# Rotary position embedding: fp16 tiles summed on TensorE, or fp32 tiles worked in place by four engines

## The chip, the cores and the metric

One core of a Trainium2 chip runs the kernel. The metric is device time in microseconds of one execution. The kernel before has a median of 165.84 us over 3 runs (165.72 to 165.95).

## What is computed

`x` is fp32 of shape (16, 512, 1024): 16 batches, 512 positions, and 16 heads of 64 values side by side. `cos` and `sin` are (512, 32). Each head's 64 values are two halves of 32, and every position's halves are rotated:

```python
x = x.reshape(batch, seq, num_heads, head_dim)
x1, x2 = x[..., :half_dim], x[..., half_dim:]
cos, sin = cos[None, :, None, :], sin[None, :, None, :]
rotated = np.concatenate([x1 * cos - x2 * sin, x1 * sin + x2 * cos], axis=-1)
```

The output is fp32 of the same size, so 33.55 MB are read and 33.55 MB written. For each element that is one product with cosine, one product of the other half with plus or minus sine, and one sum.

## The kernel before

A batch is one tile: position `4p + kk` lies on partition `p`, so a partition holds 4 positions, 16 KB in fp32. Set-up (L51 to L62) makes a 128x128 fp16 identity, loads cosine and sine from SP (L56, L57) and casts them to fp16 tables on DVE, sine twice: negated for the first half of a head, plain for the second.

The loop over `bo` (L82) takes two batches at a time. POOL issues one DMA that loads both and casts them to fp16 on the way (L84); this runs on the software queue, q0. Then for each batch:

- DVE multiplies the tile by cosine into `A` (L90), and the tile with its halves swapped (`swap_view`, a view that steps backwards by 32) by the signed sine into `Bt` (L92). Each is one operation over 128x4096 in fp16.
- PE adds the two: for each of 8 chunks of 512 columns an identity matmul of `A` (L101) and one of `Bt` (L102) accumulate in one PSUM bank, in fp32.
- ACT copies each chunk from PSUM into `o_sb` (L103), in fp32.
- SP stores `o_sb`, 2 MB, on the hardware queue, q1 (L105).

The order on each engine is the scheduler's, from the dependences and the buffers: 3 of `x_sb` (two batches each), 2 of `A` and `Bt`, 3 of `o_sb`, 4 PSUM banks. POOL's fourth load waits until DVE has read the first `x_sb`; ACT's copies for the fourth batch wait until the first store has landed.

Of the kernel before, what the change touches and what calls it, by code (L numbers as in the profile page):

```python
# [1 line left out]

# [5 lines left out]

FP32 = mybir.dt.float32  # L10
FP16 = mybir.dt.float16
ALU = mybir.AluOpType


@with_exitstack
def kernel(
    ctx: ExitStack,
    tc: tile.TileContext,
    x: bass.AP,
    cos: bass.AP,  # L20
    sin: bass.AP,
    num_heads: bass.AP,
    out: bass.AP,
):
    nc = tc.nc
    P = nc.NUM_PARTITIONS
    batch, seq, dim = x.shape
    nh = num_heads
    head_dim = dim // nh
    half = head_dim // 2  # L30

    KK = seq // P
    assert P * KK == seq
    FREE = KK * dim
    CH = 512
    assert FREE % CH == 0
    BP = 2
    assert batch % BP == 0

    x_v2 = x.rearrange("(bo bi) (p kk) d -> bo p bi kk d", bi=BP, kk=KK)  # L40
    out_v = out.rearrange("b (p kk) h d -> b p kk (h d)", kk=KK)
    cos_v = cos.rearrange("(p kk) j -> p kk j", kk=KK)
    sin_v = sin.rearrange("(p kk) j -> p kk j", kk=KK)

    fixed = ctx.enter_context(tc.tile_pool(name="fixed", bufs=1))
    xin = ctx.enter_context(tc.tile_pool(name="xin", bufs=3))
    tmp = ctx.enter_context(tc.tile_pool(name="tmp", bufs=2))
    orez = ctx.enter_context(tc.tile_pool(name="orez", bufs=3))
    psum = ctx.enter_context(tc.tile_pool(name="psum", bufs=4, space=bass.MemoryType.PSUM))

    ident = fixed.tile([P, P], FP16)  # L51
    make_identity(nc, ident)

    cos_sb = fixed.tile([P, KK, half], FP32)
    sin_sb = fixed.tile([P, KK, half], FP32)
    nc.sync.dma_start(out=cos_sb, in_=cos_v)  # L56
    nc.sync.dma_start(out=sin_sb, in_=sin_v)  # L57
    cos16 = fixed.tile([P, KK, half], FP16)
    sns16 = fixed.tile([P, KK, 2, half], FP16)
    nc.vector.tensor_copy(out=cos16, in_=cos_sb)  # L60
    nc.vector.tensor_scalar_mul(out=sns16[:, :, 0, :], in0=sin_sb, scalar1=-1.0)  # L61
    nc.vector.tensor_copy(out=sns16[:, :, 1, :], in_=sin_sb)  # L62

    cosb = bass.AP(
        tensor=cos16.tensor,
        offset=cos16.offset,
        ap=[cos16.ap[0], [half, KK], [0, nh * 2], [1, half]],
    )
    snsb = bass.AP(
        tensor=sns16.tensor,  # L70
        offset=sns16.offset,
        ap=[sns16.ap[0], [2 * half, KK], [0, nh], [1, 2 * half]],
    )

    def swap_view(x_sb):
        return bass.AP(
            tensor=x_sb.tensor,
            offset=x_sb.offset + half,
            ap=[x_sb.ap[0], [head_dim, KK * nh], [-half, 2], [1, half]],
        )  # L80

    for bo in range(batch // BP):  # L82
        x_sb = xin.tile([P, BP, KK, dim], FP16)
        nc.gpsimd.dma_start(out=x_sb, in_=x_v2[bo])  # L84
        for bi in range(BP):
            b = bo * BP + bi
            xb = x_sb[:, bi]

            A = tmp.tile([P, KK, dim], FP16, name="A")
            nc.vector.tensor_tensor(out=A, in0=xb, in1=cosb, op=ALU.mult)  # L90
            Bt = tmp.tile([P, KK, dim], FP16, name="Bt")
            nc.vector.tensor_tensor(out=Bt, in0=swap_view(xb), in1=snsb, op=ALU.mult)  # L92

            o_sb = orez.tile([P, KK, dim], FP32)
            Aflat = A.rearrange("p kk d -> p (kk d)")
            Bflat = Bt.rearrange("p kk d -> p (kk d)")
            oflat = o_sb.rearrange("p kk d -> p (kk d)")
            for c in range(FREE // CH):
                sl = slice(c * CH, (c + 1) * CH)
                ps = psum.tile([P, CH], FP32)  # L100
                nc.tensor.matmul(out=ps, lhsT=ident, rhs=Aflat[:, sl], start=True, stop=False)  # L101
                nc.tensor.matmul(out=ps, lhsT=ident, rhs=Bflat[:, sl], start=False, stop=True)  # L102
                nc.scalar.copy(out=oflat[:, sl], in_=ps)  # L103

            nc.sync.dma_start(out=out_v[b], in_=o_sb)  # L105


# [1 line left out]
_INS = ['x', 'cos', 'sin', 'num_heads']  # L109
_OUTS = [((16, 512, 16, 64), 'float32')]  # L110
#: Inputs that are plain numbers.
_NUMBERS = {'num_heads': 16}


# [26 lines left out]
```

## Time and profile before

| What | Value |
|---|---|
| Median of 3 runs | 165.84 us |
| Span of the profiled execution | 164.1 us (its time outside the span is not given) |
| Busy: PE, DVE, ACT, POOL | 88.6, 72.5, 68.7, 6.5 us |
| Largest wait on DVE | 41.3 us for the load of `x_sb` |
| Largest wait on ACT | 58.5 us for stores out of `o_sb` |
| From issue to landing: load of two batches, store of one | 40.3 us, 23.5 us (medians) |
| Last store: issued, span's end | 152.38 us, 164.1 us |

The span runs from the first instruction to the last. A transfer is counted in GB/s by the bytes that it writes; the line on HBM counts what was read and written there. The DMA line gives the mean busy share of 16 DMA engines in 40 slices of 4.1 us, in tenths. Stretches of the span are given as start and end in microseconds.

### The profile page before, as it was taken

What the parts mean: (1) busy time and instruction counts of PE and PEld (TensorE: products, weight loads), DVE (VectorE), ACT (ScalarE), POOL (GpSimd) and SP (SyncE); (2) the same over time, 40 slices, a digit from 0 to 9 for tenths busy, and PEclk for the clock granted to TensorE, in tenths of its full rate; (3) what the DMA queues carried; (4) which work ended last, traced back from release to release, by engine and by line L of the source; (5) the groups of instructions that cost most, each with busy time, mean ns of one, the idle gap of its engine ahead of it and who ended that gap; (6) DMA issues with size and microseconds to landing.
All of it is one profiled execution on the core that took longest, in us unless ns stands there. A gap on an engine that the chain in (4) does not pass through costs nothing.

```text
span 164.1 us, 814 instructions
## 1 busy us (share of the span) xinstructions
PE 88.6 (54%) x256; PEld 31.5 (19%) x256; DVE 72.5 (44%) x35; ACT 68.7 (42%) x129; POOL 6.5 (4%) x14
## 2 busy tenths in 40 slices
PE   0000599940954908639195491954919559986000
PEld 0000133310311302213032130311303123331000
DVE  1005979904880073900929037280733707950000
ACT  3000289811805409145080541806428075798100
POOL 7000010010001000010000100000000000000000
PEclk9999999998586585865858658586585855999955
DMA  5999999999999999999999999999999999999992
GB/s 90 196 218 222 220 208 180 290 332 326 312 312 330 324 298 336 306 308 346 310 312 312 326 328 306 326 308 326 326 316 316 304 403 423 413 435 443 423 423 92
DMA packets 4772, 50.51 MB, mean 308 GB/s; under 512 B 416, under 2 KB 672, under 8 KB 672
## 3 DMA queue, kind: packets, MB, share of 16 engines
q0 software_dynamic: 2176, 16.78, 49.7%
q1 hardware_dynamic: 2592, 33.69, 48.8%
q8 instruction: 2, 0.03, 0.1%
q14 instruction: 2, 0.02, 0.0%
HBM read 33.69 MB, written 33.55 MB: 410 GB/s over the span
## 4 chain that ended last, share of the span: by engine, by line
DMA 71%; PE 11%; ACT 6%; DVE 3%; issue 1%; ACTq 0%; POOL 0%; POOLq 0%; DVEq 0%
DMA out_dram<-o_sb 63%; DMA x_sb<-in_x_dram 8%; ACT o_sb L103 6%; PE ps L102 6%; PE ps L101 6%; DVE A L90 1%; DVE Bt L92 1%; ACTq L136 0%; POOL ident masks.py:197 0%; ACTq L103 0%; POOLq masks.py:199 0%; DVEq L90 0%; POOLq L122 0%
## 5 line engine op out<-in xcount | busy, mean ns | idle before, releaser
L103 ACT COPY o_sb<-ps 128x512 f32<-128x512 f32 x128 | 67.4, 609 | 82.9 <-DMA out_dram<-o_sb 58.5
L101 PE MATMUL ps<-A,ident 128*128 128x512 f16 x128 | 65.4, 519 | 60.8 <-ACT o_sb L103 43.6
L90 DVE TENSOR_TENSOR A<-x_sb,cos 128x4096 f16<-128x4096 f16 x16 | 36.7, 2291 | 69.9 <-DMA x_sb<-in_x_dram 41.3
L102 PE MATMUL ps<-Bt,ident 128*128 128x512 f16 x128 | 62.9, 506 | 1.6 <-DVE Bt L92 1.6
L92 DVE TENSOR_TENSOR Bt<-x_sb,sns 128x4096 f16<-128x4096 f16 x16 | 36.6, 2285 | 0.0
L102 PEld LDWEIGHTS <-ident 128*128 128x128 f16 x128 | 15.6, 122 | 87.0 <-issue 83.7
L101 PEld LDWEIGHTS <-ident 128*128 128x128 f16 x128 | 15.8, 124 | 32.1 <-issue 23.5
L84 POOL DMA_DIRECT2D x_sb<-in_x_dram x8 | 5.8, 730 | 83.9 <-DVE Bt L92 83.6
L103 ACT ACT_TABLE_LOAD x1 | 1.3, 1283 | 0.7 <-PEq L122 0.7
L60 DVE CAST cos<-cos_sb 128x128 f16<-128x128 f32 x1 | 0.2, 227 | 2.6 <-DMA cos_sb<-in_cos_dram 2.6
L61 DVE TENSOR_SCALAR sns<-sin_sb 128x128 f16<-128x128 f32 x1 | 0.5, 509 | 0.6 <-DMA sin_sb<-in_sin_dram 0.6
L62 DVE CAST sns<-sin_sb 128x128 f16<-128x128 f32 x1 | 0.4, 434 | 0.0
masks.py:199 POOL TENSOR_SCALAR_AFFINE_SELECT ident<-ident 128x128 f16<-128x128 f16 x1 | 0.3, 304 | 0.1
masks.py:197 POOL MEMSET ident<- 128x128 f16 x1 | 0.2, 205 | 0.3 <-POOLq L122 0.3
L122 POOL MEMSET const-float32-0.0<- 128x1 f32 x1 | 0.1, 93 | 0.2 <-issue 0.2
L122 POOL MEMSET const-bfloat16-1.0<- 128x1 bf16 x1 | 0.1, 95 | 0.0
L122 POOL MEMSET const-uint8-127<- 128x1 uint8 x1 | 0.1, 95 | 0.0
L122 POOL MEMSET const-float32-1.0<- 128x1 f32 x1 | 0.1, 93 | 0.0
## 6 DMA issues: line engine op xcount, KB each, us to landing
out_dram<-o_sb SPq DMA_DIRECT2D x16, 2048.0 KB, 23.5
x_sb<-in_x_dram POOLq DMA_DIRECT2D x8, 2048.0 KB, 40.3
cos_sb<-in_cos_dram SPq DMA_DIRECT2D x1, 64.0 KB, 1.8
sin_sb<-in_sin_dram SPq DMA_DIRECT2D x1, 64.0 KB, 2.2
```

The costliest lines, as they stand in the source:

```text
L60: nc.vector.tensor_copy(out=cos16, in_=cos_sb)
L61: nc.vector.tensor_scalar_mul(out=sns16[:, :, 0, :], in0=sin_sb, scalar1=-1.0)
L62: nc.vector.tensor_copy(out=sns16[:, :, 1, :], in_=sin_sb)
L84: nc.gpsimd.dma_start(out=x_sb, in_=x_v2[bo])
L90: nc.vector.tensor_tensor(out=A, in0=xb, in1=cosb, op=ALU.mult)
L92: nc.vector.tensor_tensor(out=Bt, in0=swap_view(xb), in1=snsb, op=ALU.mult)
L101: nc.tensor.matmul(out=ps, lhsT=ident, rhs=Aflat[:, sl], start=True, stop=False)
L102: nc.tensor.matmul(out=ps, lhsT=ident, rhs=Bflat[:, sl], start=False, stop=True)
L103: nc.scalar.copy(out=oflat[:, sl], in_=ps)
L122: nc = _bacc.Bacc("TRN2", target_bir_lowering=False, num_devices=1)
```

## The change

The new kernel keeps fp32 from end to end and writes the result over the input tile.

- **Tiles.** Two batches make one tile of 128 partitions: 64 partitions for each batch, 8 positions ("rows" of 1024 values) per partition, 32 KB. There are 8 tiles, and 5 buffers for them.
- **Transfers.** All are issued from SP on the hardware queue, in an order written out by hand: both tables, tile 0 in two halves (rows 0 to 3, rows 4 to 7), tiles 1 to 4, stores of tiles 0 to 2, loads of tiles 5 to 7, stores of tiles 3 to 6, the store of tile 7 in two halves. Each load of the second round waits for a store out of its buffer.
- **Tables.** Cosine and sine are loaded once to 64 partitions. PE copies them to both halves of 128 partitions in PSUM, through selection matrices that DVE makes from the identity (three fp32 matmuls). `sns_ps` and `cos_ps` stay in PSUM and are read there by DVE; ACT copies both to SBUF, and POOL reads the copy `sns`.
- **Rows 0 and 1** of each tile go as before: a product `B` with sine (row 0 on POOL, row 1 on DVE), a product with cosine in place (DVE), two fp32 identity matmuls for each 512 columns (PE), and a copy back over the tile (ACT). There are two `B` buffers, one for POOL and one for DVE, and two PSUM banks.
- **Rows 2 to 7** go in three pairs: POOL makes the product `T` with sine (128x2048, two buffers), DVE makes the product `pp` with cosine into PSUM (one buffer of four banks) and adds `T` and `pp` over the tile.

So DVE does per tile three operations of 128x1024 and six of 128x2048, POOL one of 1024 and three of 2048, PE 8 matmuls of 512 columns and ACT 4 copies of 512. On DVE the order is: `B` of row 1, cosine of row 1, cosine of row 0 (after POOL's `B`, which reads the row), then product and sum of each pair. Every DVE operation there has an operand in PSUM. Six of the nine wait for the operation in front of them: cosine of row 1, all sums, and the second and third product into `pp`. The matmuls of row 1 stand ahead of those of row 0.

The core of the diff (the launch is the same; shapes, views and pools are cut):

```diff
-    for bo in range(batch // BP):
-        x_sb = xin.tile([P, BP, KK, dim], FP16)
-        nc.gpsimd.dma_start(out=x_sb, in_=x_v2[bo])
-        for bi in range(BP):
...
-            nc.vector.tensor_tensor(out=A, in0=xb, in1=cosb, op=ALU.mult)
...
-            nc.vector.tensor_tensor(out=Bt, in0=swap_view(xb), in1=snsb, op=ALU.mult)
...
-                nc.tensor.matmul(out=ps, lhsT=ident, rhs=Aflat[:, sl], start=True, stop=False)
-                nc.tensor.matmul(out=ps, lhsT=ident, rhs=Bflat[:, sl], start=False, stop=True)
-                nc.scalar.copy(out=oflat[:, sl], in_=ps)
-            nc.sync.dma_start(out=out_v[b], in_=o_sb)
+    NB = 5
+    PAIRS = (2, 4, 6)
+    PEROWS = (0, 1)
+    xv = x.rearrange("b (p r) d -> (b p) (r d)", r=R)
+    xv = xv.rearrange("(t p) f -> t p f", p=P)
...
+    ctx.enter_context(tc.manual_schedule())
...
+    nc.sync.dma_start(out=tabs[:, 1], in_=sinv)
+    nc.sync.dma_start(out=tabs[:, 0], in_=cosv)
+    nc.sync.dma_start(out=x_tiles[0][:, :H], in_=xv[0][:, :H])
+    nc.sync.dma_start(out=x_tiles[0][:, H:], in_=xv[0][:, H:])
+    def load(t):
+        x_tiles[t] = xin.tile([P, R * dim], FP32, name="x_sb")
+        nc.sync.dma_start(out=x_tiles[t], in_=xv[t])
+    for t in range(1, NB):
+        load(t)
...
+    nc.tensor.matmul(out=sns_ps[:, :, 1, :], lhsT=sel[:, 0, :], rhs=sin3, start=True, stop=True)
+    nc.tensor.matmul(out=sns_ps[:, :, 0, :], lhsT=sel[:, 1, :], rhs=sin3, start=True, stop=True)
+    nc.tensor.matmul(out=cos_ps.rearrange("p r j -> p (r j)"), lhsT=sel[:, 0, :], rhs=tabs[:, 0],
+                     start=True, stop=True)
...
+    nc.scalar.copy(out=sns, in_=sns_ps)
+    nc.scalar.copy(out=cost, in_=cos_ps)
...
+    def compute(t):
+        xt = x_tiles[t]
...
+        for r in PEROWS:
+            B = bpool.tile([P, dim], FP32, name="B")
+            eng = nc.vector if r == PEROWS[-1] else nc.gpsimd
+            eng.tensor_tensor(out=B, in0=swapped(xt, r, 1), in1=snsb(sns_ps if eng is nc.vector else sns, r, 1),
+                              op=ALU.mult)
+            bs[r] = B
+        for r0 in PAIRS:
+            T = tpool.tile([P, 2 * dim], FP32, name="T")
+            nc.gpsimd.tensor_tensor(out=T, in0=swapped(xt, r0, 2), in1=snsb(sns, r0, 2), op=ALU.mult)
+            ts[r0] = T
+        for r in reversed(PEROWS):
+            xr = view(xt, r, 1)
+            nc.vector.tensor_tensor(out=xr, in0=xr, in1=cosb(cos_ps, r, 1), op=ALU.mult)
+            for c in range(2):
+                ps = prow.tile([P, dim // 2], FP32, name="ps")
+                xc = xr[:, c * dim // 2:(c + 1) * dim // 2]
+                bc = bs[r][:, c * dim // 2:(c + 1) * dim // 2]
+                nc.tensor.matmul(out=ps, lhsT=ident, rhs=xc, start=True, stop=False)
+                nc.tensor.matmul(out=ps, lhsT=ident, rhs=bc, start=False, stop=True)
+                nc.scalar.copy(out=xc, in_=ps)
+        for r0 in PAIRS:
+            pp = ppair.tile([P, 2 * dim], FP32, name="pp")
+            xr = view(xt, r0, 2)
+            nc.vector.tensor_tensor(out=pp, in0=xr, in1=cosb(cos_ps, r0, 2), op=ALU.mult)
+            nc.vector.tensor_tensor(out=xr, in0=ts[r0], in1=pp, op=ALU.add)
+    for t in range(NB):
+        compute(t)
+        if t < NT - NB:
+            nc.sync.dma_start(out=ov[t], in_=x_tiles[t])
+    for t in range(NB, NT):
+        load(t)
+    for t in range(NT - NB, NB):
+        nc.sync.dma_start(out=ov[t], in_=x_tiles[t])
+    for t in range(NB, NT):
+        compute(t)
+        if t < NT - 1:
+            nc.sync.dma_start(out=ov[t], in_=x_tiles[t])
+    nc.sync.dma_start(out=ov[NT - 1][:, :H], in_=x_tiles[NT - 1][:, :H])
+    nc.sync.dma_start(out=ov[NT - 1][:, H:], in_=x_tiles[NT - 1][:, H:])
```

## Prediction

> **What bounds the kernel now.** I read the page's 40 slices and its queue table first, then stretches of the span, then the first instructions of DVE, ACT and PE.
>
> ```profile
> DMA  5999999999999999999999999999999999999992
> ...
> q0 software_dynamic: 2176, 16.78, 49.7%
> q1 hardware_dynamic: 2592, 33.69, 48.8%
> ...
> HBM read 33.69 MB, written 33.55 MB: 410 GB/s over the span
> ```
>
> The 16 DMA engines are busy from the first slice to the last but one. The two queues add up to 98.5%. The chain of waits names PE, ACT and DVE for a quarter of the span, but these steps only hand buffers on while the transfers run. Now the same by stretches (columns: stretch and length, busy time of PE, PEld, DVE, ACT, POOL, clock, DMA share, GB/s):
>
> ```profile
> 8.00:24.00 16.00, 5.86 (x17) 2.05 (x17) 8.95 (x5) 3.58 (x7) 0.62 (x1) 1.00 1.03 215
> ...
> 72.00:102.00 30.00, 18.44 (x48) 6.43 (x48) 13.48 (x6) 12.85 (x25) 0.72 (x1) 0.67 1.02 319
> ...
> 148.00:160.00 12.00, 2.19 (x9) 0.67 (x7) 0.00 (x0) 4.01 (x8) 0.00 (x0) 0.83 1.00 427
> ```
>
> A load counts here by what it writes, in fp16. Loads alone (8 to 24) thus read HBM at 2 x 215 = 430 GB/s. Between 72 and 102 us the queues moved 3.28 MB on q0 and 6.29 MB on q1, so HBM saw (2 x 3.28 + 6.29) / 30 us = 428 GB/s. Stores alone run at 427. The rate is the same in all three, so the time is set by fp32 bytes on the HBM side: 67.24 MB / 428 = 157.1 us. **The change moves the same bytes there**: fp16 tiles had halved only the SBUF side.
>
> The rest of the 164.1 us span: finer stretches give DMA shares of 0, 0.30, 0.53, 0.91 in the half microseconds up to 3.0, which is 2.1 us lost at the start. At the end the share falls from 159 us on and is zero from 162.0, 3.5 us lost. 164.1 - 157.1 - 2.1 - 3.5 leaves 1.4 us of slower stretches (4 to 8 us: 402 GB/s of HBM; 28 to 36 us, as stores join: 393). The median run, 165.84, lies 1.7 us above the profiled span. I carry that 1.7 over.
>
> **The change, part by part.**
>
> *Transfers.* Start: SP issues the two tables (0.38 and 0.42 us from 0.74, as before), then tile 0 in halves from 1.6 us. The lost 2.1 us stay, since x starts within half a microsecond of where it does now. The 3.5 us at the end stay: the last store is again 2 MB. The 157.1 us shrink a little, by packets twice as long. Bounds: no row has a 32 KB packet. The small ones of 1 to 3 us (283 packets, 25.1% of 16 engines x 2 us) took 28 ns each, where 512 bytes at the large ones' pace would be 19, so a packet costs up to 9 ns beyond its bytes. The large ones (313 in 148 to 160, 612 ns each) would save half of that per 16 KB: 0 to 1.2 us over all. A loss is excluded by no row, but three mixes at one rate speak against it. I take 0.6. The eight issues on POOL (0.73 us each) and the cast they made vanish; they hid under the transfers, so that gives nothing. The 1.4 us of dips came where two queues met; with one queue and one direction at a time I take them as gone, and keep them as a bound. Sum: 2.1 + 157.1 - 0.6 + 3.5 = **162.1 us of span, 163.8 us**. With all the dips back and no gain by packets it is 165.8; with the whole gain 163.2. A further 1.2 us below is possible if the start or the last 3.5 us shortens, which no row excludes.
>
> *Is there always a transfer to run?* 4.19 MB take 9.8 us. On SP's queue: loads 0 to 4 until 51.4, stores 0 to 2 until 80.8, loads 5 to 7 until 110.2, stores 3 to 6 until 149.4, the two last halves until 159.2. Behind each waiting store on SP stands every later transfer. So tile t must be ready when its store's turn comes: store 0 at 51, store 2 at 71, store 3 at 110, store 6 at 140, the last halves at 149 and 154. Load 5 waits for store 0 (landed at 62), load 7 for store 2 (82); their turns are at 81 and 100.
>
> *DVE* becomes the busiest engine. The nearest rows:
>
> ```profile
> 14.18 2.29 DVE L90 TENSOR_TENSOR A<-x_sb,cos 128x4096 f16<-128x4096 f16 x1 [10.21 <-DMA x_sb<-in_x_dram]
> 16.39 2.29 DVE L92 TENSOR_TENSOR Bt<-x_sb,sns 128x4096 f16<-128x4096 f16 x1
> 18.59 2.29 DVE L90 TENSOR_TENSOR A<-x_sb,cos 128x4096 f16<-128x4096 f16 x1
> ```
>
> 8 KB per operand take 2.29 us, and one that waits for nothing starts 2.20 after the other. In fp32 these bytes are 2048 elements; by elements it would be 1.15 us, and no row gives a dearer one. I take bytes. For 1024 elements I draw a line through this and the cast of 128 fp32 elements (0.5 KB, 0.23 us): 1.19 us. A handover from DVE to PE takes 0.05 us (L90 ends at 16.47, PE starts at 16.53); the new operations wait for the one in front in 6 of 9 cases. Per tile: 1.19 + 0.05, two of 1.10, five of 2.29 + 0.05, one of 2.20: 17.3 us. It has to fit under the 19.6 us that a tile's load and store take.
>
> Start: half of tile 0 lands at 1.6 + 4.9 + about 2.2 (a table took 1.8 to 2.2 from issue to landing) = 8.7 us. The tables come earlier: sine landed by 2.9, three fp32 matmuls of 256 columns (up to four f16 passes of 0.21 each) and a copy of at most 0.59 on ACT, about 6. Tile 0 waits about 1 us for POOL's first product, so tiles end at 27.0, 44.3, 61.7, 79.0, 96.4, 113.7, 131.1, 148.4. Every store is ready before its turn. By DVE alone the span would be 148.4 + 2.0 + 4.9 + 1.3 (from the last landing to the end) = 156.6. **Cover: 162.1 - 156.6 = 5.5 us, or 76 ns on each of 72 operations.** What no row shows is PSUM as an operand of DVE, on every one of them. Bounds: nothing, to 0.15 us (ACT's copy of 512 elements out of PSUM takes 0.59, of which 0.43 is the pace of PE's cold stream of the same 512). I take 0.03. [...]
>
> *POOL* takes on 7168 of two-input elements per tile. Its rows: memset of 128 columns 205 ns, of one 93, so 0.88 ns per element; the affine select 304 ns, 1.65. Doubled for two inputs that is 3.3. From 6.3 to 23.7 us per tile; I take 2.1 ns, 15 us, between the affine select and its double. It decides from 2.5 ns (18.1 us per tile) on. [...]
>
> *PE and ACT.* 8 fp32 matmuls per tile in place of 16 f16 ones per 2 MB. A f16 one starts every 0.43 us for some 4.5 us of a burst (72.49 to 77.14) and every 0.215 later. With both operands twice as wide I take four times that: 11 x 0.43 + 21 x 0.215 = 9.2 us per tile. From 1.7 (a f16 price) to 17.7 us (all cold, a weight load of 0.124 at each of four passes). ACT copies 4 x 0.6 = 2.4 us. Both are hidden under DVE. What waits for PE is POOL's next B, by its buffer.
>
> **Rivals.**
> 1. *DVE takes the transfers' place (the slower side).* One mechanism: fixed cost of PSUM operands on DVE's 72 operations. For: no row, 9 chained operations per tile. Against: 76 ns of cover. From 0.11 us each it is slower than before; at 0.15 the span is 156.6 + 10.8 = 167.4, 169.1 us. Chance 0.14.
> 2. *POOL becomes the bound*: at 2.7 ns per element 19.4 us per tile, 8.7 + 155 + 4.7 (DVE's last two operations) + 8.2 = 176.6, 178 us. For: rows that reach to 3.3. Chance 0.08.
> 3. *PE stays cold* and at 17.7 us per tile holds POOL's B, POOL holds DVE's row 0: some 2 us more in every second tile, about 170 us. Against: the clock rose within each burst before. Chance 0.06.
> 4. *Nothing gained*: transfers cost by bytes alone, and dips come back where loads and stores meet: 165.8 us. Chance 0.12.
>
> **Numbers.** The forecast has 0.60 and its own range is 162.0 to 165.4. The measurement tells some 0.2% from no change, which is 165.5 to 166.2. Faster 0.60 (the forecast), within 0.12 (rival 4), slower 0.28 (1 to 3). The range reaches from 162.0 into rival 1 and 3, to 170.0; it leaves out POOL's bound, the dear half of rival 1 and a DMA yet faster.
>
> **What would show it.** One hardware queue with DMA 9 in all slices, near 430 GB/s, DVE at 84% or more and waiting for DMA only at the start: right. Slices with DMA under 9 late in the span, and SP waiting for DVE at stores 5 to 7: rival 1. DVE idle before its additions and POOL near 100%: rival 2. DVE idle before row 0's product, PE near 100%: rival 3. It would be wrong outright if 32 KB packets moved slower per byte than 612 ns per 16 KB.

## The result, and the profile after

| What | Before | After |
|---|---|---|
| Median | 165.78 us (6 runs, 165.56 to 165.96) | 164.59 us (6 runs, 164.35 to 165.30) |
| Span of the profiled execution | 164.1 us | 162.7 us (its time: 164.86) |
| Busy DVE, POOL, PE, ACT | 72.5, 6.5, 88.6, 68.7 us | 137.7, 127.1, 77.5, 21.0 us |

The ratio is 0.9931, with a 95% interval from 0.9913 to 0.9949: 0.7% faster, outside the 0.2% that the prediction called no change. The forecast was 163.8; of the 2.0 us it promised, 1.2 came.

First the page of the kernel after: the transfers in 40 slices, the one queue, and HBM.

```profile
DMA  4999989999899998999999999989989989999992
...
q1 hardware_dynamic: 2752, 67.24, 97.0%
...
HBM read 33.69 MB, written 33.55 MB: 413 GB/s over the span
```

One queue carries all 67.24 MB and the 16 engines stay busy, so the transfers still set the time. The rate over the span rose from 410 to 413 GB/s and no more. The scattered 8s are slices at 80 to 89%. A packet counts whole where it starts and takes 1.2 us here, so single slices scatter (371 to 508 GB/s in the middle of the page's row of GB/s), and only long stretches tell a rate.

The same by stretches of the kernel after (stretch and length, busy PE, PEld, DVE, ACT, POOL, clock, DMA share, GB/s):

```profile
2.00:2.50 0.50, 0.00 (x0) 0.00 (x0) 0.00 (x0) 0.01 (x1) 0.00 (x0) 1.00 0.34 115
2.50:3.00 0.50, 0.00 (x0) 0.00 (x0) 0.00 (x0) 0.00 (x0) 0.00 (x0) 1.00 0.54 96
...
72.00:102.00 30.00, 13.40 (x26) 5.43 (x25) 29.25 (x17) 3.91 (x7) 28.25 (x8) 0.76 1.00 433
...
4.00:156.00 152.00, 76.58 (x133) 31.49 (x131) 137.22 (x72) 19.71 (x34) 126.39 (x32) 0.76 1.00 429
148.00:151.00 3.00, 0.00 (x0) 0.00 (x0) 2.90 (x2) 0.00 (x0) 0.00 (x0) 0.66 0.86 371
144.00:152.00 8.00, 2.24 (x6) 0.69 (x4) 7.02 (x4) 1.17 (x2) 2.44 (x1) 0.81 1.00 430
```

Writes are fp32 now, so GB/s is the rate on HBM's side without doubling. Over 152 us it is 429; before, the two queues wrote 16.56 and 31.54 MB in the same stretch, (2 x 16.56 + 31.54) / 152 = 425. Nothing moves until 2.0 us, and until 3.0 what moves is the two tables (the first two rows). The row from 148 to 151, 0.86 just before the last store is issued, looks like a transfer that waits for DVE. Over 144 to 152 the share is 1.00, so nothing is lost there; 3 us are too short a stretch for packets of 1.2 us.

The groups of the kernel after that the forecast had to price without a row (count | busy, mean ns | idle time before, its releaser):

```profile
L126 POOL TENSOR_TENSOR T<-x_sb,sns 128x2048 f32<-128x2048 f32 x24 | 108.3, 4532 | 10.4 <-DVE x_sb L143 10.4
...
L143 DVE TENSOR_TENSOR x_sb<-T,pp 128x2048 f32<-128x2048 f32 x24 | 54.9, 2287 | 3.4 <-POOL T L126 1.0
L142 DVE TENSOR_TENSOR pp<-x_sb,cos_ps 128x2048 f32<-128x2048 f32 x24 | 55.0, 2293 | 0.6
...
L131 DVE TENSOR_TENSOR x_sb<-x_sb,cos_ps 128x1024 f32<-128x1024 f32 x16 | 18.8, 1218 | 0.5
L121 DVE TENSOR_TENSOR B<-x_sb,sns_ps 128x1024 f32<-128x1024 f32 x8 | 9.7, 1215 | 7.7 <-DMA x_sb<-in_x_dram 7.7
```

DVE takes 2290 ns for 2048 fp32 elements with one operand in PSUM, the time of 4096 fp16 elements out of SBUF before (2.29 us). It waits once for DMA, 7.7 us at the start, and 1.0 us in all for POOL. POOL needs 2.21 ns per element.

DVE's own order in the kernel after, from the first product to the last sum (start, length, what, idle time before):

```profile
9.55 1.22 DVE L121 TENSOR_TENSOR B<-x_sb,sns_ps 128x1024 f32<-128x1024 f32 x1 [7.68 <-DMA x_sb<-in_x_dram]
...
16.46 2.29 DVE L143 TENSOR_TENSOR x_sb<-T,pp 128x2048 f32<-128x2048 f32 x1 [1.02 <-POOL T L126]
18.79 2.29 DVE L142 TENSOR_TENSOR pp<-x_sb,cos_ps 128x2048 f32<-128x2048 f32 x1
21.18 2.29 DVE L143 TENSOR_TENSOR x_sb<-T,pp 128x2048 f32<-128x2048 f32 x1
```

```profile
148.98 2.29 DVE L143 TENSOR_TENSOR x_sb<-T,pp 128x2048 f32<-128x2048 f32 x1
```

A sum starts 0.10 us after the product that it needs (18.79 + 2.29 to 21.18), a product 0.04 after a sum. The first tile ends at 28.2 us and the others every 17.6; the last sum ends at 151.27, where 148.4 was forecast.

SP's issues in the kernel after (start, length, line):

```profile
0.73 0.54 SPq L61 DMA_DIRECT2D tabs<-in_sin_dram  x1
1.33 0.57 SPq L62 DMA_DIRECT2D tabs<-in_cos_dram  x1
1.96 0.58 SPq L63 DMA_DIRECT2D x_sb<-in_x_dram  x1
...
146.89 0.33 SPq L157 DMA_DIRECT2D out_dram<-x_sb  x1
151.29 0.33 SPq L158 DMA_DIRECT2D out_dram<-x_sb  x1
```

A table's issue takes 0.54 and 0.57 us here (0.38 and 0.42 before), so `x` is issued at 1.96, and its first packets start at 3.2.

**The loss by stretches.** At 428 GB/s 67.24 MB take 157.1 us; the rest of the span is time lost. With the bytes of each stretch, lost is its length less bytes / 428:

| Stretch | Before: MB, us lost | After: MB, us lost | Change | Forecast |
|---|---|---|---|---|
| 0 to 4 us | 0.56, 2.7 | 0.39, 3.1 | +0.4 | 0 |
| 4 to 156 us | 64.66, 0.9 | 65.21, -0.4 | -1.3 | -2.0 |
| 156 us to the end | 2.02, 3.4 | 1.64, 2.9 | -0.5 | 0 |
| Span (sum) | 164.1 us | 162.7 us | -1.4 | -2.0 |
| Time outside the span | 1.7 us | 2.2 us | +0.5 | 0 |

(The forecast's -2.0 are the 1.4 of dips and the 0.6 of packets. By this division some 0.5 of its 1.4 lies in the first 4 us, where the kernel before lost 2.7 us and not 2.1.) The question for the experiments: is it the transfers that end last, and not DVE; what made the middle faster; and what holds the start and the end.

### The profile page after: what moved, and what is told of

Read it like the earlier page. It is cut to its first block, busy times and chain, and to the rows that moved or that the text cites. A ratio compares the mean times of both kernels' runs of the same rounds, so it can differ in the third digit from the quotient of the medians.

```text
span 162.7 us, 575 instructions
## 1 busy us (share of the span) xinstructions
PE 77.5 (48%) x134; PEld 32.3 (20%) x134; DVE 137.7 (85%) x75; ACT 21.0 (13%) x35; POOL 127.1 (78%) x38
## 3 DMA queue, kind: packets, MB, share of 16 engines
q1 hardware_dynamic: 2752, 67.24, 97.0%
## 5 line engine op out<-in xcount | busy, mean ns | idle before, releaser
L126 POOL TENSOR_TENSOR T<-x_sb,sns 128x2048 f32<-128x2048 f32 x24 | 108.3, 4532 | 10.4 <-DVE x_sb L143 10.4
L136 PE MATMUL ps<-x_sb,ident 128*128 128x512 f32 x64 | 44.4, 783 | 65.7 <-issue 41.4
L143 DVE TENSOR_TENSOR x_sb<-T,pp 128x2048 f32<-128x2048 f32 x24 | 54.9, 2287 | 3.4 <-POOL T L126 1.0
L142 DVE TENSOR_TENSOR pp<-x_sb,cos_ps 128x2048 f32<-128x2048 f32 x24 | 55.0, 2293 | 0.6
L137 PE MATMUL ps<-B,ident 128*128 128x512 f32 x64 | 40.1, 713 | 0.0
L138 ACT COPY x_sb<-ps 128x512 f32<-128x512 f32 x32 | 18.8, 586 | 121.7 <-PE ps L137 120.6
L136 PEld LDWEIGHTS ps<-x_sb,ident 128*128 128x128 f32 x64 | 15.1, 251 | 87.8 <-issue 81.0
L121 POOL TENSOR_TENSOR B<-x_sb,sns 128x1024 f32<-128x1024 f32 x8 | 18.8, 2350 | 8.3 <-DMA x_sb<-in_x_dram 8.3
L137 PEld LDWEIGHTS ps<-B,ident 128*128 128x128 f32 x64 | 15.4, 240 | 21.8 <-issue 21.8
L131 DVE TENSOR_TENSOR x_sb<-x_sb,cos_ps 128x1024 f32<-128x1024 f32 x16 | 18.8, 1218 | 0.5
L121 DVE TENSOR_TENSOR B<-x_sb,sns_ps 128x1024 f32<-128x1024 f32 x8 | 9.7, 1215 | 7.7 <-DMA x_sb<-in_x_dram 7.7
```

The costliest lines, as they stand in the source:

```text
L121: eng.tensor_tensor(out=B, in0=swapped(xt, r, 1), in1=snsb(sns_ps if eng is nc.vector else sns, r, 1), op=ALU.mult)
L126: nc.gpsimd.tensor_tensor(out=T, in0=swapped(xt, r0, 2), in1=snsb(sns, r0, 2), op=ALU.mult)
L131: nc.vector.tensor_tensor(out=xr, in0=xr, in1=cosb(cos_ps, r, 1), op=ALU.mult)
L136: nc.tensor.matmul(out=ps, lhsT=ident, rhs=xc, start=True, stop=False)
L137: nc.tensor.matmul(out=ps, lhsT=ident, rhs=bc, start=False, stop=True)
L138: nc.scalar.copy(out=xc, in_=ps)
```

## The experiments

Theory: the bytes at some 429 GB/s set the end, and what is left is the start and the tail. Its main rival: DVE, which ends 2.9 us later than forecast, holds the last stores. Times are medians; the kernel before ran beside them at 165.73 (first four), 165.66 (next four) and 165.75 us (last four).

### The kernel before, unchanged (x0_before)

> The kernel before, unchanged, for its span beside its own time. The changed kernel's runs have 2.2 us outside the span (164.86 against 162.7). If the same holds here, the 1.7 us that the prediction carried over were too small by 0.5 us for both kernels, and that is part of its miss. If the kernel before has 1.7 us outside, then the change added 0.5 us there.

165.66 us in a single run with a span of 163.9, so 1.76 us lie outside the span. Another profile of before shows the same queues and the same slices, so the differences above aren't one odd execution.

### The transfers alone (x1_moves)

Out go the tables, the set-up and the whole body of `compute`:

```diff
-    nc.sync.dma_start(out=tabs[:, 1], in_=sinv)
-    nc.sync.dma_start(out=tabs[:, 0], in_=cosv)
...
-            nc.vector.tensor_tensor(out=pp, in0=xr, in1=cosb(cos_ps, r0, 2), op=ALU.mult)
-            nc.vector.tensor_tensor(out=xr, in0=ts[r0], in1=pp, op=ALU.add)
```

> All loads and stores of x in the changed kernel's order, without tables and without any computation: the output is x, unrotated. Theory (transfers set the end): 161.5 to 163.5 us, that is 164.6 less the tables at the start (0.5 to 1 us) and the dip of 0.4 us at 148 to 151 us of the span. Rival (DVE sets the end): without DVE it falls to the bare transfers; by the share of 97.0% of 162.7 us, 157.8 us of packets and some 4 us at both ends, that would still be near 162, so what tells them apart is the end: by the rival the last store's transfers begin at least 2 us earlier than in the changed kernel, by the theory less than 1 us earlier beyond the start's gain.

161.78 us, ratio 0.9762 (0.9746 to 0.9778). The slices and queue of this kernel:

```profile
DMA  5999999999999999999999999999999999999895
...
q1 hardware_dynamic: 2592, 67.11, 98.2%
```

And its stretches (stretch and length, busy POOL, clock, DMA share, GB/s):

```profile
1.50:2.00 0.50, 0.00 (x0) 1.00 1.70 360
...
4.00:156.00 152.00, 0.00 (x0) 1.00 1.00 430
148.00:151.00 3.00, 0.00 (x0) 1.00 0.83 355
...
158.00:159.00 1.00, 0.00 (x0) 1.00 0.24 98
```

Between 4 and 156 us the bare transfers run at 430, the full kernel at 429: **all of the computing costs the transfers almost nothing there.** The row from 148 to 151 is low here too (0.83), with nothing computed and the last store issued by 112 us. So it shows no wait, and reading it as rival 1 would have been wrong. What the full kernel costs beyond its transfers is 2.8 us: the first packets of `x` start at 1.7 us in place of 3.2, and in this ruler the start loses 2.3 us (after: 3.1), the last stretch 1.6 (after: 2.9). The sign that was to tell the two apart speaks for the theory: in the trace the first packet of the store of tile 7 starts at 148.5, in the kernel after at 149.9. That is 1.4 us earlier, no more than the start's gain; by the rival it would be 2 us or more.

One place in the middle is slower in both, where the first stores follow the loads of the first round. First the bare transfers, then the kernel after:

```profile
44.00:60.00 16.00, 0.00 (x0) 1.00 0.98 397
```

```profile
44.00:60.00 16.00, 9.65 (x16) 3.90 (x16) 15.69 (x9) 2.34 (x4) 14.49 (x4) 0.71 1.02 418
```

Against 428 GB/s that is 1.1 and 0.4 us lost, on one queue. The kernel before lost 0.9 us in the same situation: from 24 to 36 us, as its first stores joined, HBM saw 4.76 MB (1.65 on q0, twice, and 1.46 on q1), 397 GB/s. From 36 to 128 us, where both its queues ran all the time, it saw 39.43 MB, 429 GB/s, and lost nothing.

### Each transfer in four DMAs, packets of 8 KB (x2_quarters)

```diff
-        nc.sync.dma_start(out=x_tiles[t], in_=xv[t])
+        for k in range(4):
+            nc.sync.dma_start(out=x_tiles[t][:, k * Q:(k + 1) * Q], in_=xv[t][:, k * Q:(k + 1) * Q])
...
-        nc.sync.dma_start(out=ov[t], in_=x_tiles[t])
+        store(t)
```

> The changed kernel with each whole load and store cut into four DMAs of a quarter of the columns: packets of 8 KB in place of 32 KB, the same bytes in the same order. Theory (a packet has a fixed cost of about 9 ns beyond its bytes): 4 x 128 packets more per engine on 14 of 16 moves, about 3 x 112 x 9 ns = 3.0 us more, 167.6 us. Rival (bytes alone set the pace): within 0.3 us of 164.6.

166.26 us, ratio 1.0032 (1.0020 to 1.0044): 1.7 us over the kernel after, where the price per packet asked for 3.0. A packet of 8 KB takes 311 ns, one of 32 KB mostly 1213, one of 16 KB took 612 before. So four cost 31 ns more than one large. The cut meets 14 of the 16 moves, 112 large packets per engine, so that would be 3.5 us. The pages' totals give 2.6 (97.7% of 164.2 us against 97.0% of 162.7), and 1.7 showed in the time. The stretch from 4 to 156 us:

```profile
4.00:156.00 152.00, 76.67 (x133) 31.52 (x131) 137.24 (x72) 19.68 (x34) 126.40 (x32) 0.78 1.01 424
```

424 GB/s, with DVE unchanged. Packets of 8 KB in place of 32 cost more than the whole gain of the change; the direction of the forecast's term is confirmed. Cutting to a quarter adds three further packets where there was one. Halving adds one, so 16 KB should cost about 1.7 / 3 = 0.6 us by this run: an estimate, and the value that the forecast took. From 60 to 128 us, a stretch with loads and stores in all three kernels, the rates are 425 here, 428 in the kernel before (packets of 8 and 16 KB) and 431 in the kernel after. The run also makes four transfers of one. Each transfer ends with a small packet per engine, which takes 9 ns in the trace, so 42 transfers more are 0.4 us of the 2.6; no run changes the packets alone.

### One more product on DVE per tile (x3_dve_more)

```diff
             eng.tensor_tensor(out=B, in0=swapped(xt, r, 1), in1=snsb(sns_ps if eng is nc.vector else sns, r, 1),
                               op=ALU.mult)
+            if eng is nc.vector:
+                eng.tensor_tensor(out=B, in0=swapped(xt, r, 1), in1=snsb(sns_ps, r, 1), op=ALU.mult)
```

> The changed kernel with one DVE operation more per tile: the product B of row 1 is made twice, 1.25 us each time, 10.0 us over 8 tiles. The last sum would end at about 161.3 us in place of 151.3. With nothing left in the queue then, the end comes 2.0 + 4.9 + 1.3 = 8.2 us later, span 169.5, 171.7 us: 7.1 us more, and the missing 2.9 us are the cover that DVE had. Rival (DVE sets the end already, no cover): 10 us more, 174.6. If DVE was far from the bound: less than 6 us more.

170.35 us, ratio 1.0282 (1.0264 to 1.0300). The last sum of this kernel, and the stretch before it ended:

```profile
158.33 2.29 DVE L145 TENSOR_TENSOR x_sb<-T,pp 128x2048 f32<-128x2048 f32 x1
```

```profile
152.00:155.00 3.00, 3.00 (x9) 1.33 (x7) 2.90 (x2) 1.17 (x2) 3.00 (x1) 1.00 0.00 0
```

DVE ends 9.35 us later (160.62 against 151.27), the time grows by 5.76: **the cover was 3.6 us**, not the forecast's 5.5. From 152 to 157 us no byte moves, and from the last sum to the end of the span it takes 7.9 us (11.4 in the kernel after, where the last store stands behind others). This is how it looks when DVE does bind: a share of 0.00, not of 0.86, and over 5 us.

### The tables issued from ACT (x4_tables_act)

```diff
-    nc.sync.dma_start(out=tabs[:, 1], in_=sinv)
-    nc.sync.dma_start(out=tabs[:, 0], in_=cosv)
+    nc.scalar.dma_start(out=tabs[:, 1], in_=sinv)
+    nc.scalar.dma_start(out=tabs[:, 0], in_=cosv)
```

> The changed kernel with the two table loads issued from ACT in place of SP, so that tile 0 is SP's first transfer. Theory (transfers set the end, and what they lost against the forecast is their late start: x begins at about 3.0 us of the span in the changed kernel and at 1.5 without tables): x begins 1.2 to 1.5 us earlier, and the end moves with it: 163.1 to 163.5 us. Rival (the end is set by DVE, which waits for half of tile 0): the same gain, but then the last sum ends as much earlier and the queue is empty before the last store; by the theory it is not. Second rival (the tables delay DVE now): DVE's first product starts no earlier and nothing is gained.

163.32 us, ratio 0.9863 (0.9844 to 0.9883): 1.27 us less than the kernel after. Its stretches, and DVE's first and last operation:

```profile
1.50:2.00 0.50, 0.00 (x0) 0.00 (x0) 0.35 (x3) 0.06 (x1) 0.00 (x0) 1.00 2.13 426
...
144.00:152.00 8.00, 4.10 (x10) 1.52 (x8) 7.76 (x4) 1.76 (x3) 4.45 (x1) 0.92 0.85 365
```

```profile
11.55 1.22 DVE L121 TENSOR_TENSOR B<-x_sb,sns_ps 128x1024 f32<-128x1024 f32 x1 [9.67 <-ACT sns L94]
```

```profile
150.99 2.29 DVE L143 TENSOR_TENSOR x_sb<-T,pp 128x2048 f32<-128x2048 f32 x1
```

`x` flows 1.5 us earlier. The tables now land 8.0 and 10.7 us after their issue (2.2 and 2.3 in the kernel after), while the packets of `x` flow beside theirs; that these hold them up is an estimate of mine. DVE waits for ACT's copy of the sine, so it starts and ends 2.0 us later. **DVE later, and the time shorter**: in the kernel after the transfers set the end. Here DVE does, against what I expected of the queue: 144 to 152 falls from 1.00 to 0.85, 1.2 us of transfers, and from the last sum (153.28) to the end of the span it takes 7.8 us, as in x3_dve_more. So a start that serves both may give more.

### Loads of the second round from a second hardware queue (x5_loads_act)

```diff
-    def load(t):
+    def load(t, eng=nc.sync):
...
+        if t >= 2:
+            load(t + 3, nc.scalar)
```

> The changed kernel with the loads of tiles 5 to 7 issued from ACT, each after ACT's copies of tiles 2 to 4, so that loads and stores run on two hardware queues at once between 63 and 115 us of the span. The forecast took it that two queues meeting cost 1.4 us of dips. Theory (they do): packets of 32 KB above 1.22 us in that stretch, about 1 us more, 165.6. Rival (two directions at once cost nothing, and what made the packets of the kernel before longer is the software queue with its cast): within 0.3 us of 164.6.

164.33 us, ratio 0.9918 (0.9905 to 0.9932), which overlaps the kernel after. Loads and stores from two queues at once, from 63 to 115 us, first with two queues, then the kernel after with one:

```profile
63.00:115.00 52.00, 29.68 (x48) 12.01 (x48) 50.70 (x28) 7.04 (x12) 46.72 (x13) 0.70 1.00 433
```

```profile
63.00:115.00 52.00, 27.47 (x48) 11.27 (x48) 50.70 (x28) 7.03 (x12) 46.69 (x13) 0.76 1.00 431
```

433 against 431 GB/s, and a packet of 32 KB keeps 1.21 us: two hardware queues that meet cost nothing here. The prediction's reason for the dips of before falls for hardware queues. Its own row from 72 to 102 us spoke against it too: both queues of the kernel before ran there, at 428.

### Each second-round load right behind its store (x6_interleave)

```diff
         nc.sync.dma_start(out=ov[t], in_=x_tiles[t])
+        if t < NT - NB:
+            load(t + NB)
```

(The stores of tiles 0 to 4 stand in one loop, and the separate loop of loads goes.)

> The changed kernel without its two rounds: on SP the load of tile 5 stands right behind the store of tile 0, that of 6 behind the store of 1, that of 7 behind the store of 2. Each load waits for the store in front of it to land, and the next store stands behind the load. Theory (the order of two rounds is what keeps the queue filled): three times about 2.7 us of an empty queue (1.2 from the last data to the landing, 1.5 from issue to first data), 8 us more less what the stores catch up, 170 to 173 us. Rival (the order does not matter, the bytes do): within 0.5 us of 164.6.

175.74 us, ratio 1.0609 (1.0593 to 1.0626): 11.2 us over the kernel after, more than expected. The wait of SP, a store behind it, and the transfers at that time:

```profile
64.12 0.33 SPq L68 DMA_DIRECT2D x_sb<-in_x_dram  x1
64.56 0.36 SPq L147 DMA_DIRECT2D out_dram<-x_sb  x1
```

```profile
60.00:64.00 4.00, 0.00 (x0) 0.00 (x0) 3.90 (x3) 0.00 (x0) 4.00 (x2) 0.73 0.65 279
...
84.00:88.00 4.00, 4.00 (x6) 1.55 (x5) 3.90 (x3) 0.59 (x1) 3.36 (x1) 0.50 0.48 205
```

Load 5 needs the buffer of store 0, and SP stands still from 28.7 to 64.1 us until that has landed. The stores behind it are ready and not issued, and the queue runs dry: 0.65 and 0.48. Two rounds avoid it, because three stores lie in the queue while the first lands. That is the prediction's queue table, shown from its other side.

### First-round loads from POOL (x7_pool_loads)

```diff
     for t in range(1, NB):
-        load(t)
+        load(t, nc.gpsimd)
```

> One look: the changed kernel with the loads of tiles 1 to 4 issued from POOL, so on the software queue, in fp32 without a cast. It tells what lengthened the packets of the kernel before. If it is the software queue, the 32 KB packets of these loads take 1.24 us and more where only they run (8 to 28 us); if it is the packet length or the cast, 1.21 to 1.22 us as on the hardware queue. Time: within 1 us of 164.6, since these loads are issued at about the same time.

183.88 us in a single run: the expectation, within 1 us, missed by 19. Where this kernel waits (engine, waiting line, for whom: us in total, times, longest):

```profile
DVE B L121 <- DMA x_sb<-in_x_dram: 20.7, 1, 20.7
...
DVE pp L142 <- DMA x_sb<-in_x_dram: 5.4, 1, 5.4
```

I had thought of bytes alone. The halves of tile 0 share the engines with 16 MB that POOL issued beside them: they land 30.4 us after their issue in place of 9.6 (medians). DVE's first wait grows from 7.7 to 20.7 us, and a second of 5.4 follows, for the other half. Its last sum ends at 174.64, 23.4 us later than in the kernel after; less the cover of 3.6 that is 19.8, near the 19.3 that were measured. So DVE, now late, sets the end. The question that the run was for, whether the software queue itself is slower, it answers in part: from 28 to 50 us q0 moved 8.00 MB in fp32 at 84.4% of the engines' time, 1217 ns per 32 KB packet, as on q1. So the queue isn't slow by itself; what its cast costs no run shows.

### Half of the first half ahead of the tables (x8_rows_first)

```diff
+    Q = H // 2
+    nc.sync.dma_start(out=x_tiles[0][:, :Q], in_=xv[0][:, :Q])
     nc.sync.dma_start(out=tabs[:, 1], in_=sinv)
     nc.sync.dma_start(out=tabs[:, 0], in_=cosv)
-    nc.sync.dma_start(out=x_tiles[0][:, :H], in_=xv[0][:, :H])
+    nc.sync.dma_start(out=x_tiles[0][:, Q:H], in_=xv[0][:, Q:H])
```

> The changed kernel with SP's first transfers in another order: rows 0 and 1 of tile 0, then both tables, then rows 2 and 3, then rows 4 to 7, the rest as it was. Theory (transfers set the end, DVE follows with 3.6 us of cover): x begins at 1.5 us in place of 3.0 with nothing ahead of it, the tables land at about 5.2 and DVE begins at about 8.4, not 9.55 as in the changed kernel nor 11.55 as with the tables on ACT. So the queue stays filled to the end and the whole 1.5 us are won: 162.6 to 163.1 us, below the 163.3 of the tables on ACT. Rival (the end hangs on DVE): 163.4, that is 1.2 us less, by DVE's earlier start.

164.08 us, ratio 0.9893 (0.9873 to 0.9914): 0.5 us under the kernel after (the intervals just touch), and 1.0 us above the range that I expected. The first packets of `x` start at 1.7 us and DVE's last sum ends at 150.8, so the start was better for both, and yet:

```profile
158.00:159.00 1.00, 0.00 (x0) 0.00 (x0) 0.00 (x0) 0.00 (x0) 0.00 (x0) 0.50 0.39 164
159.00:160.00 1.00, 0.00 (x0) 0.00 (x0) 0.00 (x0) 0.00 (x0) 0.00 (x0) 0.50 0.12 49
```

The engines run dry from 158 us on (after: 0.95 from 158 to 159), and a few packets straggle until 161. In the ruler of the loss by stretches the start wins 0.9 us and the middle 0.3, and the tail loses 0.7. Why the engines end unevenly isn't shown.

### The two together (x9_rows_first_act)

The edit of x8_rows_first, and loads 5 to 7 on ACT's queue:

```diff
+    nc.sync.dma_start(out=x_tiles[0][:, :Q], in_=xv[0][:, :Q])
     nc.sync.dma_start(out=tabs[:, 1], in_=sinv)
...
+        if t >= 2:
+            load(t + 3, nc.scalar)
```

> The kernel with rows 0 and 1 first, and besides the loads of tiles 5 to 7 issued from ACT as tried before, where 0.26 us were won. If that was real, SP no longer waits for landings and 0.2 to 0.3 us come on top; if it was scatter between chips, the same time as without it, within 0.15 us.

163.71 us, ratio 0.9870 (0.9850 to 0.9890). Its interval overlaps that of x8_rows_first and that of x4_tables_act; the three can't be ranked. All three lie under the kernel after by 0.5 to 1.3 us, and in all three the first packets of `x` start at 1.7 us.

### POOL's products taken out (x10_no_pool)

```diff
+    Tc = fixed.tile([P, 2 * dim], FP32, name="Tc")
+    nc.gpsimd.memset(Tc, 0.5)
...
+            if r != PEROWS[-1]:
+                bs[r] = Tc[:, :dim]
+                continue
...
-            nc.gpsimd.tensor_tensor(out=T, in0=swapped(xt, r0, 2), in1=snsb(sns, r0, 2), op=ALU.mult)
-            ts[r0] = T
+            ts[r0] = Tc
```

> The changed kernel without POOL's products: a constant tile, written once, stands for T and for B of row 0, so the output lacks the products with sine on rows 0 and 2 to 7. DVE, PE, ACT and all transfers do what they did. Theory (POOL is under DVE and does not slow it): DVE's operations keep 2.29 and 1.22 us, a tile keeps 17.5, the first tile ends about 1 us earlier, and the time stays within 0.4 us of 164.6. Rival (POOL and DVE share a way into SBUF): DVE's operations get shorter and its last sum ends more than 3 us earlier. It also shows whether the 2.2 us outside the span, 1.8 in the kernel before, come with POOL's products.

164.92 us, ratio 0.9944 (0.9928 to 0.9960), no better than the kernel after. The sum in this kernel:

```profile
L146 DVE TENSOR_TENSOR x_sb<-Tc,pp 128x2048 f32<-128x2048 f32 x24 | 54.9, 2286 | 0.8
```

2286 ns with POOL idle, 2287 with POOL busy for 78% of the span: the operations of the kernel after don't disturb each other. DVE's last sum ends at 148.73, 2.5 us earlier, and the time doesn't follow. I expected 1 us: the first tile ends 1.1 us earlier, and each sum starts 0.04 us after its product and not 0.10, which makes the rest. So the longer handover goes with the second thing that a sum waits for, POOL's product. This is x4_tables_act from the other side: **DVE isn't the bound.** The time outside the span, 2.19 us, isn't POOL's either.

### The product `pp` in SBUF in place of PSUM (x11_pp_sbuf)

```diff
-    ppair = ctx.enter_context(tc.tile_pool(name="ppair", bufs=1, space=bass.MemoryType.PSUM))
+    psb = ctx.enter_context(tc.tile_pool(name="psb", bufs=1))
...
-            pp = ppair.tile([P, 2 * dim], FP32, name="pp")
+            pp = psb.tile([P, 2 * dim], FP32, name="pp")
```

Must sums that read both their inputs from SBUF and POOL's products take turns?

> The changed kernel with the product pp in SBUF in place of PSUM, so that each sum on DVE reads two tiles from SBUF. It undoes one part, the intermediate in PSUM. [...] If so, three sums of 2.29 us and POOL's 15.9 us per tile can't overlap: at least 22.8 us per tile, 9.5 + 8 x 22.8 + 8.2 + 2.2 = 202 us. Without contention: the same 164.6 us, and sums of 2.29 us.

210.19 us, ratio 1.2678 (1.2656 to 1.2700), above 202, the least that I expected if the two can't overlap. The groups of this kernel:

```profile
L126 POOL TENSOR_TENSOR T<-x_sb,sns 128x2048 f32<-128x2048 f32 x24 | 108.3, 4516 | 43.1 <-DVE x_sb L143 43.1
L143 DVE TENSOR_TENSOR x_sb<-T,pp 128x2048 f32<-128x2048 f32 x24 | 104.3, 4345 | 3.4 <-POOL T L126 1.0
...
L142 DVE TENSOR_TENSOR pp<-x_sb,cos_ps 128x2048 f32<-128x2048 f32 x24 | 54.8, 2284 | 0.5
...
L121 POOL TENSOR_TENSOR B<-x_sb,sns 128x1024 f32<-128x1024 f32 x8 | 33.2, 4145 | 8.4 <-DMA x_sb<-in_x_dram 8.4
```

Only the sum now has both inputs in SBUF, and only the sum (2287 to 4345 ns) and a POOL product that meets it (`B`, 2350 to 4145) grow; the product with cosine, its table still in PSUM, stays at 2284. The means mix sums that met POOL and sums that didn't. One after the other (start, length):

```profile
70.59 4.52 POOL L126 TENSOR_TENSOR T<-x_sb,sns 128x2048 f32<-128x2048 f32 x1 [3.58 <-DVE x_sb L143]
...
72.94 4.32 DVE L143 TENSOR_TENSOR x_sb<-T,pp 128x2048 f32<-128x2048 f32 x1
...
75.08 4.40 POOL L121 TENSOR_TENSOR B<-x_sb,sns 128x1024 f32<-128x1024 f32 x1
```

```profile
198.26 2.29 DVE L143 TENSOR_TENSOR x_sb<-T,pp 128x2048 f32<-128x2048 f32 x1
```

The sum at 72.94 starts inside POOL's `T` and ends at 77.26, 2.15 us after `T` has ended. `B`, which starts inside that sum, ends 2.22 us after it. The last sum of the kernel, with POOL done, takes 2.29 us. So here one waits until the other is through. With `pp` in PSUM, in the kernel after, the two run side by side and keep their times (the sum 2287 ns, `T` 4532 ns). The place of `pp` is worth 45.6 us. The PSUM operands that the prediction feared as rival 1 are what keeps this division of rows under the transfers.

## Why the prediction was right, and where its sizes failed

The direction and the mechanism held: the transfers bound both kernels, and the change took lost time from them. What failed are sizes: 0.8 us in the sum, 164.59 against 163.8. Of it 0.3 us lie in the span of the median run (162.4 against 162.1) and 0.5 outside it. That the span came so near is partly luck: in the profiled run the start is 1.0 us dearer than its term (3.1 against 2.1), the middle 0.2, and the end 0.6 cheaper (2.9 against 3.5).

- **157.1 us of bytes at 428 GB/s: right.** 429 from 4 to 156 us, 430 with nothing but transfers.
- **"The lost 2.1 us stay, since x starts within half a microsecond": mis-sized.** The half microsecond held: the first packets of `x` start at 3.2 us in place of 2.8. But the 2.1 went by the DMA share, which counts the tables' small packets as busy; by bytes the first 4 us lost 2.7 before, and they lose 3.1 now. I took the table issues "as before" at 0.38 and 0.42. They take 0.54 and 0.57, and before, `x` had its own issuer, POOL, and didn't stand behind them. What lengthens an issue isn't shown: that of `x` behind the tables takes 0.58 too, and 0.37 with nothing ahead of it (x1_moves). The load that moved to SP's queue took on all that stood ahead of it there.
- **The end, 3.5 us, "stays": too dear by 0.5** (3.4 to 2.9 in one ruler), which the forecast kept as a bound. It isn't fixed: 1.6 with transfers alone, some 2.0 in x4_tables_act.
- **Packets, 0.6 of 0 to 1.2: size supported** by 1.7 us for two halvings down to 8 KB, and by the steady rates: 425, 428 and 431 GB/s.
- **"The 1.4 us of dips came where two queues met; I take them as gone": wrong in the reason, half right in the size.** The middle gave 1.3 us in all. Of these some 0.8 are a higher rate outside the dips, and some 0.5 a smaller dip where the first stores join: 0.9 us from 24 to 36 us before (0.6 in x0_before), 0.4 from 44 to 60 after. This dip comes on one queue too (1.1 us with the transfers alone), and two queues that go on together lost nothing, before (429 GB/s from 36 to 128 us) or with loads on ACT's queue (433). So the number of queues doesn't make it. With packets of 8 KB it is nearly gone (424 from 44 to 60, 425 from 60 to 128); its cause stays open.
- **1.7 us outside the span "carried over": wrong by 0.5.** It is about 1.8 in before and in the transfers alone, 2.2 in the kernel after, and 1.9 to 2.3 in the variants that compute. Its cause is open; POOL's products are excluded (2.19 without them).
- **DVE 17.3 us per tile, cover 5.5 us: 17.6 and 3.6.** The chained sums wait 0.10 us and not 0.05, the start is 0.85 later. Being under the transfers, this cost nothing: without POOL DVE ended 2.5 us earlier, and nothing was gained. "By bytes" for fp32 was right: 2290 ns for 8 KB per operand.
- **PSUM +0.03 us: zero.** 1215 to 1218 ns for 1024 elements and 2287 to 2293 for 2048 leave 1.05 ns per element and 0.14 us fixed. The last sum of x11_pp_sbuf, out of SBUF alone and beside no work of POOL, took the same 2.29 us, and the fp16 product out of SBUF 2291 ns.
- **POOL 2.1 ns per element: 2.21, 15.9 us per tile.** Its products take 4532 ns for 2048 elements and 2350 for 1024. With DVE at 17.6 us per tile POOL is off the path: taking its work out gained nothing (164.92 us in x10_no_pool).
- **PE 9.2 us per tile: 9.3** (74.6 us from 8 to 160), under DVE. The factor of four was an estimate; in the kernel after fp32 matmuls of 512 columns start 1.70 us apart early in a burst (32.52, 34.22) and 0.86 later (72.47, 73.33), four times the 0.43 and 0.215 of before.

The rivals: 1 falls by the two PSUM rows; 2 by 2.21 ns against the 2.5 from which POOL would decide; 3 by 9.3 us against 17.7; 4, nothing gained, by a ratio whose interval ends at 0.9949. Rival 4 came nearest: had the packets been short, x2_quarters shows, nothing would have been left (1.0032).

**A faster version:** with the tables on ACT's queue the kernel takes 163.32 us, 1.4% under before. The transfers alone take 161.78, so 1.5 us are left to a start that brings tables and `x` early together (DVE is the bound in that version), to the tail, and to what lies outside the span. No run here got them.

## What to carry to other kernels

When the transfers bound a kernel at a fixed rate, price a change by the length of its packets, which moved the steady rate from 425 to 431 GB/s here, and by the bytes moved in the first and the last few microseconds. A load that changes its queue inherits every issue that stands ahead of it (`x` was issued at 1.26 us from POOL before, at 1.96 behind the tables after). Whether an engine near the bound really ends last is told by making it later or earlier and watching the time (x4_tables_act, x10_no_pool), not by a dip of 3 us in the DMA share (0.86), which the bare transfers showed as well (0.83). And keep on one in-order queue nothing that must wait in front of what is ready: in x6_interleave SP stood still from 28.7 to 64.1 us, and the time grew by 11.2 us.

## What the runs showed of the hardware

- **DVE and POOL took turns in x11_pp_sbuf:** sums with both inputs in SBUF took 4345 ns in the mean beside POOL's products, 2.29 us when POOL was done, and 2287 ns with one input in PSUM; one buffer's place made 45.6 us.
- **The cost of a packet** was about 10 ns beside its bytes (8 KB 311, 16 KB 612, 32 KB 1213 ns), and part of it vanished: 2.6 us of engine time showed as 1.7.
- **Transfers beside larger ones on another queue landed late:** the 64 KB tables landed 8.0 and 10.7 us after issue in place of 2.2 and 2.3, and with 16 MB beside it on the software queue the first half of tile 0 kept DVE waiting for 20.7 us in place of 7.7.
- **Two hardware queues cost nothing against one** (433 and 431 GB/s), and a software queue without a cast moved its packets as fast (1217 against 1213 ns).
- **Open:** the dip where the first stores join, the uneven end of the 16 engines, and the 0.5 us outside the span.
